# Opening of a hybrid attention/mLSTM diffusion step: x loaded, normalised and transposed ahead of the modulation weights, and modulated three row blocks at a time from SBUF

## The chip, the cores and the metric

The kernel runs on one core of a Trainium2 chip. TensorE (PE) multiplies matrices and transposes, VectorE (DVE), ScalarE (ACT) and GpSimd (POOL) do elementwise work, and SyncE (SP) issues nearly all transfers between HBM and SBUF. The metric is device time of one execution in microseconds, given as the median of several runs. Beside the timed runs there is one profiled execution, from which all rows of the profile come.

## The reference, cut to what matters

One layer of a diffusion backbone works on 128 context tokens and 1024 latent tokens of width 1024: nine row blocks of 128 tokens. The parts which the change touches are the first ones:

```python
m = jax.nn.silu(cond) @ w_ada_l + b_ada_l              # six rows of 1024: sh1, sc1, g1, sh2, sc2, g2
h = rmsnorm(x, norm1_w) * (1 + sc1) + sh1              # context tokens use c_ctx, latent tokens use c
aq, ak, av, mq, mk, mv, mo, mg = jnp.split(h @ w_in, SPLIT_POINTS, axis=-1)
```

Behind them come attention over context and latent keys, a bidirectional mLSTM of four heads over chunks of 128 tokens, a merged output projection, and a SwiGLU feed-forward of width 2816. All arithmetic is in float32.

## The kernel before, in words

The nine row blocks (block 0 is the context, blocks 1 to 8 the latent tokens) are grouped three to a chunk c, so that c=0 holds blocks 0, 1, 2. Everything multiplies from a transposed layout: `hT[c]` holds h of three blocks with the 1024 features over eight groups k of 128 partitions, split into an f16 high part `hTh` and an f16 low part `hTl`, and weights are split likewise into pairs; three f16 products then stand for one float32 product.

The opening goes as follows.

- Small rows (c, c_ctx, biases, norm weights) are loaded on ACT's queue and transposed; SiLU gives `silp` (L286 to L301).
- SP loads block 0 of x (L268) and then sixteen tiles of 512 KB of the modulation weights w_ada (L273): eight for the shift, eight for the scale. They lie in a pool of their own, `awp`, which is closed behind them. Then come the cached keys and values and the gate bias (L377 to L379), the raw weights of the key/value/gate projection `kvg` (L194, tile `kraw`), blocks 1 to 8 of x (L393, L395), and the raw weights of head 0 (L194, tile `iraw`).
- `normalise` squares a block on ACT (L331), takes the reciprocal root by three Newton steps of small DVE operations (`rsqrt`, L125 to L131), and multiplies x in place on DVE (L334). `transposed` turns a block on PE into two PSUM banks of four 128-column pieces each (L114). Block 0 goes through both before the modulation weights are read.
- For shift and then for scale PE multiplies `silp` with each of the eight tiles (L318, into `wi`), two evictions (L356) and small products (L324) bring the result into columns, and `modulation` adds the bias and multiplies the norm weight (L310, L313). Then a bound over scale and shift is made a power of two (`hsc`, L364 to L366 and L162 to L165), and both are multiplied with it (L369).
- For each block in turn, eight pieces of 128 columns are read from PSUM, multiplied by scale and shifted into a tile `full`: k = 1, 4, 7 on ACT (L417), the others on DVE (L420). Each half block is cast to f16 (half 0 on ACT, L426; half 1 on DVE, L428), and POOL subtracts to give the low part (L135, `sub`).
- `Scaled` prepares a weight: `ready` loads it, takes absolute sums on ACT (L199), reduces them (L201), multiplies the bound with `hsc` (L202), and lets `power_scale` find a power of two through a PE transpose and a PE broadcast (L172 to L177). `pairs` then makes high and low parts: ACT scales and casts (L216, or L219 and L220), DVE (L217) or POOL (L135) makes the low part. For kvg this is emitted behind block 0 with a priority of 300, all low parts on DVE.
- `linear_tok` is the projection: for each group of blocks, eight k and three products (L488 to L490). For kvg it runs over five groups, `PAIRS`, with 272 columns, and `evac_kvg` writes keys, values and gates (L497, L498, L501). The preparation of head 0 (`steps`) is woven among it, 8 steps over 40 units. Behind it follows `head_project` of head 0 (L748 to L750 for q, by two chunks and then one).

The shared weight pool `wp` has tags with fixed numbers of buffers: `raw` 2, `whi` 5 and `wlo` 5, of 4 KB a partition each. Raw weights of the heads take `wlo`, finished pairs take `whi`.

The code gives only a program order and priorities. A planner simulates a timeline of the program and fixes each engine's order from it, so each engine runs its own list in order and waits on semaphores where the list says so. `hot(n)` raises the priority of what is emitted within it. What is emitted earlier usually comes earlier, but the planner may exchange operations which are ready at other times.

Of the kernel before, what the change touches and what calls it, by code (L numbers as in the profile page):

```python
# [22 lines left out]
NB = 9  # L23
# [22 lines left out]
def hybrid_step(ctx: ExitStack, tc: tile.TileContext, I: dict, O: dict):  # L46
# [55 lines left out]
    def bank():  # L102
        return psum["mm"].tile([P, 512], F32, name=nm("mm"), tag="mm")
# [76 lines left out]
    class Scaled:  # L180
# [5 lines left out]
        def ready(self):  # L186
# [15 lines left out]
            dve.tensor_tensor(out=t[:, 4:5], in0=t[:, 4:5], in1=hsc[:, 3:4], op=ALU.mult)  # L202
            yield from power_scale(gp, one1, t[:, 4:5], t[:, 6:8])
            dve.tensor_tensor(out=t[:, 8:9], in0=t[:, 6:7], in1=hsc[:, 3:4], op=ALU.mult)
            dve.tensor_scalar(out=t[:, 9:10], in0=t[:, 7:8], scalar1=P ** -0.5, scalar2=None, op0=ALU.mult)
            dve.tensor_scalar(out=t[:, 10:11], in0=t[:, 7:8], scalar1=0.5, scalar2=None, op0=ALU.mult)
            self.scale, self.inv, self.inv_k, self.inv_half = t[:, 8:9], t[:, 7:8], t[:, 9:10], t[:, 10:11]

        def pairs(self, dve_every=2):
            out = []  # L210
# [45 lines left out]
    es_w = ExitStack()  # L256
    awp = es_w.enter_context(tc.tile_pool(name="awp", bufs=1, side="right", reuse_waits="tile"))
# [9 lines left out]
    xs = [p0.tile([P, D], F32, name=f"x{b}") for b in range(NB)]  # L267
    dma(xs[0], xrow(0))  # L268
    ada_w = [[], []]
    for n in range(2):  # L270
        for k in range(KD):
            aw = awp.tile([P, D], F32, name=f"aw0_{n}_{k}")
            dma(aw, w_ada[k * P : (k + 1) * P, n * D : (n + 1) * D])  # L273
            ada_w[n].append(aw)
# [52 lines left out]
    def normalise(b0, n):  # L327
        ssx = p0.tile([P, CB], F32, name=f"ssx{b0}")
        for i in range(n):
            jk = p0.tile([P, D], BF16, name=nm("jk"), tag="jk", bufs=2)  # L330
            act(jk, xs[b0 + i], AF.Square, accum_out=ssx[:, i : i + 1])  # L331
        rs = rsqrt(p0, ssx[:, 0:n], n, 1.0 / D)
        for i in range(n):
            dve.tensor_scalar(out=xs[b0 + i], in0=xs[b0 + i], scalar1=rs[:, i : i + 1], scalar2=None, op0=ALU.mult)  # L334

    def transposed(b):
        pss = []
        for half in range(2):
            ps = bank()
            for j in range(4):  # L340
                k = half * 4 + j
                transpose(ps[:, j * P : (j + 1) * P], xs[b][:, k * P : (k + 1) * P])
            pss.append(ps)
        return pss

    normalise(0, 1)
    xT = [transposed(0)]

    for n, out in ((0, shift1), (1, scale1)):
        halves = [bankA(), bankA()]  # L350
        for k in range(KD):
            for j, pe in enumerate(halves):
                strip_products(pe, k, silp, ada_w[n][k][:, j * 512 : (j + 1) * 512], 2 * j)
        for j, pe in enumerate(halves):
            part = p0.tile([P, 512], F32, name=nm("part"), tag="part", bufs=2)
            (nc.scalar.copy if j == 0 else dve.tensor_copy)(part, pe)  # L356
            cols_from_strips(out, n, j, part, bankA)
    es_w.close()

    hp = ctx.enter_context(tc.tile_pool(name="hp", bufs=1, side="right", reuse_waits="tile"))  # L360
    hT = [hp.tile([P, 2, KD, CT], F16, name=f"hT{c}", tag=f"b{3 + c}") for c in range(NCH)]
    hTh, hTl = [t[:, 0] for t in hT], [t[:, 1] for t in hT]

    dve.tensor_reduce(out=hs2, in_=shift1, axis=AX.XY, op=ALU.max, apply_absolute_value=True)  # L364
    dve.tensor_reduce(out=hsc[:, 0:1], in_=scale1, axis=AX.XY, op=ALU.max, apply_absolute_value=True)
    dve.scalar_tensor_tensor(out=hsc[:, 0:1], in0=hsc[:, 0:1], scalar=float(D) ** 0.5, in1=hs2, op0=ALU.mult, op1=ALU.add)  # L366
    powers(hsc, P)
    for t in (scale1, shift1):
        dve.tensor_scalar(out=t, in0=t, scalar1=hsc[:, 2:3], scalar2=None, op0=ALU.mult)  # L369
    es_h = ExitStack()  # L370
    kvp = es_h.enter_context(tc.tile_pool(name="kvp", bufs=1, side="right", reuse_waits="tile"))
# [4 lines left out]

    dma(kall[:, 8], I["cache_k"][0, 0])  # L377
    dma(vall[:, 8], I["cache_v"][0, 0])
    dma(gbias, I["gate_bias"].rearrange("o g h -> o (g h)").to_broadcast([P, 16]))  # L379
    dve.memset(G, 0.0)  # L380

    Gv = G.rearrange("p t (d x) -> p d t x", d=2)

    def rows_of(j):
        return w_in[2 * j * P : (2 * j + 2) * P, :].rearrange("(a p) n -> p a n", p=P)

    kvg = Scaled([[(lambda v: v[:, :, 0:256], rows_of(j)[:, :, 512:768]),
                   (lambda v: v[:, :, 256:272], rows_of(j)[:, :, 2816:2832])] for j in range(4)], (2, 272),
                 [p0.tile([P, 544], F32, name=f"kraw{j}") for j in range(4)])
    kvg_steps = kvg.ready()  # L390
    next(kvg_steps)
    for b in range(1, CB):
        dma(xs[b], xrow(b))  # L393
    for b in range(CB, NB):
        dma(xs[b], xrow(b))  # L395
# [4 lines left out]

    groups_in = [head_group(h) for h in range(NH)] + [Scaled([[(full_view, rows_of(j)[:, :, 0:512])] for j in range(4)], (2, 512))]
    steps = groups_in[0].ready()
    next(steps)
    for c in range(NCH):
        if c > 0:
            normalise(c * CB, CB)
        for i in range(CB):
            b = c * CB + i
            cnd = 0 if b == 0 else 1
            if b in (1, 2):  # L410
                normalise(b, 1)
            for half, ps in enumerate(xT[b] if b < 1 else transposed(b)):
                full = p0.tile([P, 4, P], F32, name=nm("full"), tag="full", bufs=3)
                for j in range(4):
                    k = half * 4 + j
                    if k in (1, 4, 7):
                        act(full[:, j, :], ps[:, j * P : (j + 1) * P], AF.Identity,  # L417
                            scale=scale1[:, k, cnd : cnd + 1], bias=shift1[:, k, cnd : cnd + 1])
                    else:
                        dve.tensor_scalar(  # L420
                            out=full[:, j, :], in0=ps[:, j * P : (j + 1) * P],
                            scalar1=scale1[:, k, cnd : cnd + 1], scalar2=shift1[:, k, cnd : cnd + 1],
                            op0=ALU.mult, op1=ALU.add)
                hi = hTh[c][:, half * 4 : half * 4 + 4, i * P : (i + 1) * P]
                if half == 0:
                    nc.scalar.copy(hi, full)  # L426
                else:
                    dve.tensor_copy(hi, full)  # L428
                sub(hTl[c][:, half * 4 : half * 4 + 4, i * P : (i + 1) * P], full, hi, "pool")
            if b == 0:  # L430
                with hot(300):
                    emit(kvg_steps)
                    kvg_pairs = kvg.pairs(1)
# [69 lines left out]
    weave(linear_tok(kvg_pairs, 0, 272, evac_kvg), steps, 40, 8)  # L503
# [1016 lines left out]
```

## Time and profile before

| what | value |
|---|---|
| median of 3 runs (lowest, highest) | 1628.43 us (1624.75, 2519.12) |
| the profiled execution's own time | 1623.65 us |
| its span, first to last instruction | 1621.9 us |
| mean granted TensorE clock | 0.973 |
| busy in the span: PE, DVE, ACT, POOL | 1513.3, 955.2, 730.7, 602.4 us |
| moved by DMA | 232.71 MB |

In rows of the timeline the columns are start in us, duration in us, engine, line and operation, output and inputs, count, and in brackets the idle time before it with what ended it. In grouped rows the last columns are busy time in us, mean duration in ns, and idle time before with its releasers. In rows of one tile or line the three numbers behind the count are the smallest, median and largest duration in ns. In rows of stretches each engine has its busy time and, in brackets, its instructions; behind them stand the granted clock, the DMA engines' mean busy share and GB/s. Durations of neighbouring operations on one engine overlap a little, since an operation starts before the one ahead has been drained; the distance between starts is then the cost.

### The profile page before, as it was taken

What the parts mean: (1) busy time and instruction counts of PE and PEld (TensorE: products, weight loads), DVE (VectorE), ACT (ScalarE), POOL (GpSimd) and SP (SyncE); (2) the same over time, 40 slices, a digit from 0 to 9 for tenths busy, and PEclk for the clock granted to TensorE, in tenths of its full rate; (3) what the DMA queues carried; (4) which work ended last, traced back from release to release, by engine and by line L of the source; (5) the groups of instructions that cost most, each with busy time, mean ns of one, the idle gap of its engine ahead of it and who ended that gap; (6) DMA issues with size and microseconds to landing.
All of it is one profiled execution on the core that took longest, in us unless ns stands there. A gap on an engine that the chain in (4) does not pass through costs nothing. (4 is left out here: it accounts for less than half of the span.)

```text
span 1621.9 us, 23339 instructions
## 1 busy us (share of the span) xinstructions
PE 1513.3 (93%) x8688; PEld 1256.2 (77%) x8688; DVE 955.2 (59%) x1887; ACT 730.7 (45%) x1251; POOL 602.4 (37%) x363
## 2 busy tenths in 40 slices
PE   5899999899679867999999999999999999999996
PEld 2755666576347656998989999898898989899995
DVE  3844355847876667577663546777664474332445
ACT  3744343444444455545643344565552453333332
POOL 0411021413343414443445354443344444544443
PEclk8899999999889979999999999999999999999998
DMA  9345363302245755777763556787684445535441
GB/s 353 121 143 134 99 143 63 97 6 44 87 163 120 194 119 113 172 184 177 183 174 115 148 153 215 189 179 177 153 185 126 130 141 177 150 124 149 143 129 67
DMA packets 386311, 232.71 MB, mean 143 GB/s; under 512 B 169910, under 2 KB 346502, under 8 KB 386198
## 3 DMA queue, kind: packets, MB, share of 16 engines
q1 hardware_dynamic: 384342, 228.04, 52.6%
q10 hardware_dynamic: 1856, 3.19, 0.6%
q8 instruction: 68, 1.11, 0.3%
q14 instruction: 45, 0.37, 0.1%
HBM read 181.16 MB, written 11.69 MB: 119 GB/s over the span
## 5 line engine op out<-in xcount | busy, mean ns | idle before, releaser
L135 POOL TENSOR_TENSOR wlo<-raw,whi 128x1024 fp32r<-128x1024 f32 x146 | 360.9, 2476 | 435.6 <-ACT whi L152 404.5
L152 ACT CAST whi<-raw 128x1024 fp32r<-128x1024 f32 x219 | 224.1, 1025 | 357.9 <-DMA raw<-in_w_gu_dram 126.8
L1288 PE MATMUL mm<-aTl,whi 128*128 128x384 f32 (+2 forms) x1088 | 363.6, 334 | 0.7 <-POOL aTl L135 0.7
L1289 PE MATMUL mm<-aTh,wlo 128*128 128x384 f32 (+2 forms) x1088 | 363.4, 334 | 0.0
L1287 PE MATMUL mm<-aTh,whi 128*128 128x384 f32 (+2 forms) x1088 | 362.2, 335 | 0.8 <-DVE tn L1315 0.8
L1288 PEld LDWEIGHTS mm<-aTl,whi 128*128 128x128 f32 x1088 | 204.9, 188 | 1.7 <-POOL aTl L135 0.9
L1287 PEld LDWEIGHTS mm<-aTh,whi 128*128 128x128 f32 x1088 | 204.5, 188 | 2.2 <-DVE tn L1315 1.4
L1289 PEld LDWEIGHTS mm<-aTh,wlo 128*128 128x128 f32 x1088 | 204.9, 188 | 0.2
L135 DVE TENSOR_TENSOR wlo<-raw,whi 128x1024 fp32r<-128x1024 f32 (+1 forms) x73 | 86.7, 1188 | 145.5 <-ACT whi L152 145.3
L1106 PE MATMUL mm<-whi,hl 128*128 128x512 f32 x372 | 147.0, 399 | 1.4 <-DVE tn L1315 1.3
L1107 PE MATMUL mm<-wlo,hl 128*128 128x512 f32 x372 | 147.6, 398 | 0.0
L1108 PE MATMUL mm<-whi,hl 128*128 128x512 f32 x372 | 144.7, 397 | 0.7 <-POOL hl L135 0.7
L1023 DVE SCALAR_TENSOR_TENSOR pl<-pr,st,ph 128x1152 f16<-128x1152 f32 (+1 forms) x72 | 111.9, 1556 | 52.7 <-ACT ph L1022 51.0
L1019 ACT ACTIVATE pr<-S,st 128x1152 f32<-128x1152 f32 (+1 forms) x72 | 81.2, 1128 | 114.8 <-DVE st L1018 108.5
L488 PE MATMUL wi<-ipair,hT 128*128 128x384 f16 (+2 forms) x392 | 127.5, 326 | 2.9 <-ACT ipair L216 2.8
L489 PE MATMUL wi<-ipair,hT 128*128 128x384 f16 (+2 forms) x392 | 127.4, 325 | 0.0
L490 PE MATMUL wi<-ipair,hT 128*128 128x384 f16 (+2 forms) x392 | 126.8, 324 | 0.0
L135 POOL TENSOR_TENSOR hl<-tn,hl 128x384 fp32r<-128x384 f32 x66 | 82.8, 1256 | 106.9 <-ACT hl L1319 106.0
L1096 DVE TENSOR_TENSOR x<-x,t 128x512 f32<-128x512 f32 x102 | 116.7, 1167 | 0.8
L1315 DVE SCALAR_TENSOR_TENSOR tn<-tn,mm 128x384 f32<-128x384 f32 (+2 forms) x68 | 36.7, 540 | 136.3 <-PE mm L1289 93.5
L1016 PE MATMUL S<-kst,qT 128*128 128x384 f32 (+1 forms) x400 | 87.2, 353 | 13.5 <-ACT pr L1019 13.4
L1018 DVE TENSOR_REDUCE st<-S 128x1 f32<-128x1152 f32 (+1 forms) x72 | 88.8, 1233 | 16.7 <-PE S L1016 16.5
(353 smaller groups left out, 2639.5 us busy)
## 6 DMA issues: line engine op xcount, KB each, us to landing
raw<-in_w_gu_dram SPq DMA_DIRECT2D x132, 512.0 KB
raw<-in_w_down_dram SPq DMA_DIRECT2D x60, 512.0 KB
a<-in_w_ada_dram SPq DMA_DIRECT2D x32, 512.0 KB
gl<-g_d SPq DMA_DIRECT2D x36, 256.0 KB
aw<-in_w_ada_dram SPq DMA_DIRECT2D x16, 512.0 KB
iraw<-in_w_in_dram SPq DMA_DIRECT2D x32, 256.0 KB
raw<-in_w_out_dram SPq DMA_DIRECT2D x15, 512.0 KB
x<-in_x_sample_dram SPq DMA_DIRECT2D x13, 512.0 KB
```

The costliest lines, as they stand in the source:

```text
L135: (dve if eng == "dve" else pool).tensor_tensor(out=out, in0=full, in1=hi, op=ALU.subtract)
L152: nc.scalar.copy(hi[:, :n], raw[:, :n])
L488: mm(ps[:, :n], ah, wh[:, k % 2, c0 : c0 + n], start=(k == 0), stop=False)
L489: mm(ps[:, :n], ah, wl[:, k % 2, c0 : c0 + n], start=False, stop=False)
L490: mm(ps[:, :n], al, wh[:, k % 2, c0 : c0 + n], start=False, stop=(k == KD - 1))
L1096: eng.tensor_tensor(out=x1[:, cs], in0=x1[:, cs], in1=t, op=ALU.add)
L1106: mm(ps, ah, wh[:, k % 2, :], start=(k == 0), stop=False)
L1107: mm(ps, ah, wl[:, k % 2, :], start=False, stop=False)
L1108: mm(ps, al, wh[:, k % 2, :], start=False, stop=(k == nk - 1))
L1287: mm(ps, wh[:, k, :], th[:, k, :], start=(k == 0), stop=False)
L1288: mm(ps, wh[:, k, :], tl[:, k, :], start=False, stop=False)
L1289: mm(ps, wl[:, k, :], th[:, k, :], start=False, stop=(k == KD - 1))
```

## The change

- SP loads x in chunks of three blocks: chunks 0 and 1 (six blocks) ahead of all modulation weights, chunk 2 behind the raw kvg weights, into six x buffers instead of nine. The cached keys and values and the gate bias come behind chunk 2.
- The pool `awp` is gone. The sixteen modulation weight tiles go into `wp`: the first five into `wlo`, the next five into `whi`, two into `raw`, and the last four into `whi` again, so that these four wait for earlier tiles to be read.
- `turned(c)` takes the place of `normalise` and `transposed`: three squares, one rsqrt chain for three blocks, and per block the multiplication, eight transposes and two evictions (half 0 on ACT, half 1 on DVE) into `xT[c]` in SBUF. `turned(0)` is emitted ahead of the shift, `turned(1)` between shift and scale, `turned(2)` behind the modulation of c=1.
- `modulated(c)` multiplies and shifts `xT[c]` in place: for c=0 two pieces per k (128 columns with the context's values, 256 with the latent's) on DVE; for c=1 and c=2 one piece of 384 columns per k, k = 3 and 7 on ACT, the others on DVE. Then, per half, one cast of 1536 columns on ACT and one subtraction of 1536 columns, on POOL for half 1 of c=1 and c=2, on DVE otherwise.
- The bound `hsc` has a priority of 60, `modulated(0)` of 40; the priority of 300 at the kvg pairs is gone.
- The power of two of a weight no longer has `hsc` in it; the new method `inverse` multiplies `hsc` into the factor of the evictions.
- The kvg projection runs over six groups of blocks, and `steps` is woven over 48 units.

```diff
-            dve.tensor_tensor(out=t[:, 4:5], in0=t[:, 4:5], in1=hsc[:, 3:4], op=ALU.mult)
             yield from power_scale(gp, one1, t[:, 4:5], t[:, 6:8])
-            dve.tensor_tensor(out=t[:, 8:9], in0=t[:, 6:7], in1=hsc[:, 3:4], op=ALU.mult)
...
+            self.scale, self.t = t[:, 6:7], t
+        def inverse(self):
+            t = self.t
+            dve.tensor_tensor(out=t[:, 8:9], in0=t[:, 7:8], in1=hsc[:, 3:4], op=ALU.mult)
...
-    dma(xs[0], xrow(0))
...
+    def load_x(c):
+        xs = [p0.tile([P, D], F32, name=nm("x"), tag="x", bufs=2 * CB) for _ in range(CB)]
+        for i in range(CB):
+            dma(xs[i], xrow(c * CB + i))
+        return xs
+    def load_ada(n):
+        tiles = []
         for k in range(KD):
-            aw = awp.tile([P, D], F32, name=f"aw0_{n}_{k}")
+            tag, bufs = (("wlo", 5), ("whi", 5), ("raw", 2), ("whi", 5))[(0, 0, 0, 0, 0, 1, 1, 1, 1, 1, 2, 2, 3, 3, 3, 3)[n * KD + k]]
+            aw = wp.tile([P, 1024], F32, name=nm("aw"), tag=tag, bufs=bufs)
             dma(aw, w_ada[k * P : (k + 1) * P, n * D : (n + 1) * D])
...
+    xs = [load_x(0), load_x(1), None]
+    ada_w = [load_ada(0)]
...
+    def turned(c):
+        ssx = p0.tile([P, CB], F32, name=f"ssx{c}")
+        for i in range(CB):
             jk = p0.tile([P, D], BF16, name=nm("jk"), tag="jk", bufs=2)
+            act(jk, xs[c][i], AF.Square, accum_out=ssx[:, i : i + 1])
+        rs = rsqrt(p0, ssx, CB, 1.0 / D)
+        xT = hp.tile([P, KD, CT], F32, name=nm("xT"), tag=f"b{c}")
+        for i in range(CB):
+            dve.tensor_scalar(out=xs[c][i], in0=xs[c][i], scalar1=rs[:, i : i + 1], scalar2=None, op0=ALU.mult)
+            for half in range(2):
+                ps = bank()
+                for j in range(4):
+                    k = half * 4 + j
+                    transpose(ps[:, j * P : (j + 1) * P], xs[c][i][:, k * P : (k + 1) * P])
+                (nc.scalar.copy if half == 0 else dve.tensor_copy)(
+                    xT[:, half * 4 : half * 4 + 4, i * P : (i + 1) * P], ps.rearrange("p (j x) -> p j x", j=4))
+            yield
+        xTs.append(xT)
...
+    xTs = []
+    emit(turned(0))
+    ada_w.append(load_ada(1))
+    emit(ada_cols(0, shift1))
+    emit(turned(1))
+    kvg_steps = kvg.ready()
+    next(kvg_steps)
+    xs[2] = load_x(2)
...
+    steps = groups_in[0].ready()
     next(steps)
+    emit(ada_cols(1, scale1))
+    with hot(60):
...
+    def modulated(c):
+        xT = xTs[c]
+        for half in range(2):
+            ks = slice(half * 4, half * 4 + 4)
+            for k in range(half * 4, half * 4 + 4):
+                for lo, hi, cnd in ((0, P, 0), (P, CT, 1)) if c == 0 else ((0, CT, 1),):
+                    v = xT[:, k, lo:hi]
+                    if c > 0 and k % 4 == 3:
+                        act(v, v, AF.Identity, scale=scale1[:, k, cnd : cnd + 1], bias=shift1[:, k, cnd : cnd + 1])
                     else:
+                        dve.tensor_scalar(out=v, in0=v, scalar1=scale1[:, k, cnd : cnd + 1], scalar2=shift1[:, k, cnd : cnd + 1],
+                                          op0=ALU.mult, op1=ALU.add)
+            nc.scalar.copy(hTh[c][:, ks], xT[:, ks])
+            sub(hTl[c][:, ks], xT[:, ks], hTh[c][:, ks], "pool" if c > 0 and half == 1 else "dve")
+    with hot(40):
+        modulated(0)
+    emit(kvg_steps)
+    kvg_pairs = kvg.pairs(1)
+    modulated(1)
+    emit(turned(2))
+    modulated(2)
     es0.close()
...
-    weave(linear_tok(kvg_pairs, 0, 272, evac_kvg), steps, 40, 8)
+    weave(linear_tok(kvg_pairs, 0, 272, evac_kvg, [(0, 1), (2,), (3, 4), (5,), (6, 7), (8,)]), steps, 48, 8)
```

More of the change, by code (lines that the diff above doesn't have):

```diff
@@ L353, in hybrid_step @@
                 strip_products(pe, k, silp, ada_w[n][k][:, j * 512 : (j + 1) * 512], 2 * j)
+            yield
         for j, pe in enumerate(halves):
@@ L357, in hybrid_step @@
             cols_from_strips(out, n, j, part, bankA)
[L358 to L371, printed above, removed]
+        yield
     kall = kvp.tile([P, 10, NKV, HD], F32, name="kall")
```

95 lines of the change are left out of this document (25 added, 70 removed).

## The prediction, on record before the result

> **What bounds the kernel now.** I read the page's 40 slices first: TensorE (PE) is 90% busy or more in most slices; less so in the first two and in a few between 280 and 650 us. The change touches only what happens before the first head's projection, which is slices 1 and 2, so I then read busy time by stretches of that opening, then the timeline and the groups by line inside it.
>
> ```profile
> PE   5899999899679867999999999999999999999996
> ...
> 0.00:20.00 20.00, 12.91 (x67) 4.79 (x69) 5.84 (x30) 3.23 (x5) 1.01 (x7) 1.00 0.90 352
> ...
> 33.50:39.60 6.10, 0.97 (x4) 0.68 (x4) 5.76 (x32) 6.10 (x14) 2.20 (x2) 0.50 1.02 410
> 39.60:45.20 5.60, 4.45 (x20) 3.27 (x20) 5.57 (x20) 5.60 (x12) 0.08 (x1) 0.50 1.10 357
> 45.20:50.00 4.80, 2.95 (x24) 2.17 (x22) 4.70 (x22) 4.80 (x13) 1.16 (x1) 0.99 1.10 328
> 55.00:60.00 5.00, 2.93 (x19) 2.11 (x18) 4.94 (x17) 2.43 (x7) 0.89 (x1) 0.89 0.11 30
> 60.00:65.00 5.00, 5.00 (x36) 3.92 (x34) 4.05 (x10) 3.19 (x8) 3.59 (x4) 0.77 0.02 3
> ```
>
> The columns are the stretch, its length, busy time of PE, of its weight load, of DVE, ACT and POOL, the granted clock and DMA. From 33.5 to 60 DVE is busy in all but a few tenths, while PE is idle for long parts or runs at half clock (0.50). From 60 on PE is full. So the opening is set by the arrival of the modulation weights until about 30 us, by DVE until about 60, and by PE after it.
>
> ```profile
> 78.98 0.28 PE L490 MATMUL wi<-ipair,hT 128*128 128x272 f16 x1
> ...
> 82.45 0.28 PE L490 MATMUL wi<-ipair,hT 128*128 128x272 f16 x1
> 82.57 0.33 PE L748 MATMUL wi<-hT,ipair 128*128 128x384 f16 x1
> ```
>
> 82.57 us is the point I count to: the last matmul of the key/value/gate projection (kvg) is followed at once by the first of head 0. Behind it PE is 90% busy or more until 280 us, so what moves this point moves the end by about as much. Between the two L490 rows lie 30 matmuls: 3.47/30 = 0.1157 us each at full clock. The projection has 9 blocks x 8 x 3 = 216, hence 25.0 us. It now takes from 39.58 to 82.57, 43.0 us. The rest is 64 transposes of x, half clock, and idle time.
>
> **The change, part by part. (a) The order of the loads.** Five x tiles come ahead of the modulation weights, and all these loads share SP's queue.
>
> ```profile
> 4.96 1.06 ACT L331 ACTIVATE jk<-x 128x1024 bf16<-128x1024 f32 x1
> ...
> 25.84 1.05 PE L318 MATMUL wi<-aw,silp 128*32 128x512 f32 x4 [0.31 <-DMA aw<-in_w_ada_dram]
> ...
> 29.61 0.17 DVE L310 TENSOR_TENSOR scale<-wi,bcol 128x8 f32<-128x8 f32 x1 [0.53 <-PE wi L324]
> ...
> 31.37 0.66 ACT L199 ACTIVATE jk<-kraw 128x544 bf16<-128x544 f32 x1 [0.37 <-DMA kraw<-in_w_in_dram]
> ...
> 32.15 0.16 DVE L201 TENSOR_REDUCE isc<-isc 128x1 f32<-128x4 f32 x1 [2.38 <-ACT jk L199]
> 32.22 0.16 DVE L313 TENSOR_TENSOR scale<-scale,ncol 128x8 f32<-128x8 f32 x1
> ...
> 33.52 0.23 DVE L369 TENSOR_SCALAR shift<-shift,hsc 128x16 f32<-128x16 f32 x1
> 33.66 0.15 DVE L202 TENSOR_TENSOR isc<-isc,hsc 128x1 f32<-128x1 f32 x1
> ...
> 37.19 0.14 DVE L177 COPY isc<-mm 128x2 f32<-128x2 f32 x1
> ```
>
> The first x is there at 4.96, the sixteenth weight tile at 25.84: 1.305 us for a tile of 512 KB. Five more in front put the last weight tile at 32.4. Today the scaled vectors are ready 7.9 us after it, at 33.75; but between 29.78 and 32.15 DVE stood behind L201, whose reduction waited for the kvg weights. The new code puts the maximum of scale and shift ahead with a priority of 60 and no longer makes the kvg scale depend on it, so I take that 2.3 us out: 32.4 + 5.6 = 38.0. If L201 still goes first, 40.3. Modulation therefore starts 4.2 us later than now (bounds: 0.3 later if the planner leaves x3 to x5, 3 x 1.3 us, behind the weights, and 6.5 if L201 goes first). The reuse of weight tiles costs nothing: the last four wait until PE has read the sixth to ninth tile, which land at 11.5 + 6 x 1.305 = 19.3 up to 23.2, while their own turn in the queue begins at 11.5 + 12 x 1.305 = 27.2; that slack of about 7 us is the cover, and each us beyond it would move 38.0 by as much. The x6 to x8, cache and iraw loads come later by at most the same 6.5, and land before c=2 and head 0 need them.
>
> **(b) What leaves the stage.** Squares, rsqrt, normalising and 48 of the 72 transposes now lie in the time when PE and DVE wait for weights. Before 30 us DVE is busy 5.84 of the first 20 us, so the 12 us added there (two rsqrt chains of 1.9, 6 x 0.75, 6 half evictions) fit. New are 18 evictions from PSUM to xT, 512 wide, like L356 at 0.69 us on DVE and 0.59 on ACT; 12 of them are hidden in the same way.
>
> ```profile
> L420 DVE TENSOR_SCALAR full<-mm,scale,shift 128x128 f32<-128x128 f32 x45 | 16.2, 400 | 0.4 <-POOL hT L135 0.4
> L428 DVE CAST hT<-full 128x512 f16<-128x512 f32 x9 | 6.7, 749 | 0.6 <-ACT full L417 0.4
> L334 DVE TENSOR_SCALAR x<-x,ry 128x1024 f32<-128x1024 f32 x8 | 5.7, 750 | 0.0
> L217 DVE SCALAR_TENSOR_TENSOR ipair<-kraw,isc,ipair 128x544 f16<-128x544 f32 x4 | 3.1, 776 | 0.0
> ...
> L356 DVE COPY part<-wi 128x512 f32<-128x512 f32 x2 | 1.4, 692 | 12.2 <-PE wi L318 12.2
> L535 DVE TENSOR_SCALAR gb<-ga 128x128 f32<-128x128 f32 x1 | 0.2, 227 | 0.3 <-ACT ga L534 0.3
> L709 DVE TENSOR_SCALAR mwh<-mwh 128x512 f32<-128x512 f32 x1 | 0.4, 418 | 0.0
> L135 DVE TENSOR_TENSOR wlo<-raw,whi x73: 684/1225/1560, 458.2 to 1588.5; 128x1024 fp32r<-128x1024 f32 x67, 128x512 fp32r<-128x512 f32 x6
> L220 ACT CAST ipair<-iraw 128x1024 f16<-128x1024 f32 x2 | 2.1, 1030 | 0.0
> ```
>
> **(c) The modulation from SBUF.** The 72 pieces of 128 columns from PSUM, 45 of them on DVE and 27 (k = 1, 4, 7) on ACT, become, per c: for c=0 eight pairs of 128 and 256 columns on DVE, for c=1 and 2 six DVE and two ACT pieces of 384. From SBUF, 128 columns took 0.227 us (L535) and 512 took 0.418 (L709), so 256 is 0.29 and 384 is 0.36. That is 8 x 0.52 = 4.2, and 6 x 0.36 = 2.1 for each of the others, against 16.2 now. The nine DVE casts of 6.7 us go to ACT: six of 1536 columns at 1.03 x 1.5, or 1.5 each. Four of six subtractions go from POOL to DVE: 1.225 us at 1024 and 0.684 at 512 give 1.77 at 1536, 7.1 in all. DVE after 38.0 is then: modulation 8.4, subtractions 7.1, kvg low parts 3.1, kvg scale 1.5 (ten of 0.15), rsqrt (twelve of 0.16), normalising and evictions of c=2 1.9 + 2.3 + 2.1, gates and head 0's scale some 4.6 (32 small operations of about 0.14, the shortest above): 31 us, where it is now busy 16.0 of the 16.5 us from 33.5 to 50, 4.9 of 5 from 55 and 4.05 of 5 from 60. DVE is done at about 69, ahead of PE, so it ceases to be the bound.
>
> **(d) When kvg can start and end.** In c=0 the DVE modulates until 42.2, and subtracts the two halves until 45.7. The kvg weights land at 31.37 now, 5.5 us behind the last modulation weight, so at 37.9; 0.85 for the last absolute sum, 3.7 for the scale (L202 at 33.66 to L177's end at 37.33), ACT's high part of 0.74 and DVE's 0.78: the first pair is whole between 44 (DVE takes it between the subtractions) and 46.5 (behind them). I take 46, because modulated(0) alone has the raised priority.
>
> ```profile
> 39.58 0.39 PE L488 MATMUL wi<-ipair,hT 128*128 128x272 f16 x1 [2.79 <-ACT ipair L216]
> ...
> 42.88 0.43 PE L489 MATMUL wi<-ipair,hT 128*128 128x272 f16 x1
> ...
> 43.56 0.43 PE L489 MATMUL wi<-ipair,hT 128*128 128x272 f16 x1
> ...
> 44.01 0.43 PE L488 MATMUL wi<-ipair,hT 128*128 128x272 f16 x1
> ...
> 66.19 0.60 PE L114 MATMUL mm<-ident,x 128*128 128x128 f32 x4
> 66.63 0.28 PE L490 MATMUL wi<-ipair,hT 128*128 128x272 f16 x1
> ...
> 81.35 1.15 ACT L216 ACTIVATE ipair<-iraw,isc 128x1024 f16<-128x1024 f32 x1
> ...
> 82.53 5.28 DVE L217 SCALAR_TENSOR_TENSOR ipair<-iraw,isc,ipair 128x1024 f16<-128x1024 f32 x2 [3.42 <-ACT ipair L216]
> ```
>
> From there PE has 25.0 for kvg, 24 transposes of c=2 at 0.11 (four from 66.19 to 66.63), 2.6, head 0's scale 0.5, and a cold start: after an idle stretch the matmuls lie 0.225 apart (43.56 to 44.01); the stretches above show a clock of 0.50 from 33.5 to 45.2 and 0.99 behind it, so some 4 us after the first transposes at 41 were slow, and 4 us cost 2.0. 46 + 30.1 = 76.1. For waits on c=1 and c=2 I add 1.0 (none to 7.0, see the rivals): 77.1, 5.5 us before 82.57. The groups become six; the last is block 8 alone, so the first kvg pair gives its buffer back 2.1 us before head 0 instead of 4.2. Head 0 needs its second pair 2.0 us after its start and that pair costs 1.15 on ACT and up to 2.7 on DVE: just in time, nothing added, at worst 1 us.
>
> The profiled execution took 1623.65 us, 1.75 around its span of 1621.9. 1623.65 - 5.5 = **1618 us**. The median shown, 1628.43, is 4.8 above that execution, and the lowest run, 1624.75, 1.1 above: the spread is nearly the size of the gain. A change of 2% is about what a measurement of this kernel can tell from none.
>
> **The rivals. A larger gain.** The pairs come at 44, transposes of c=2 fall into PE's wait before that, and c=1 and 2 are always ready: 44 + 25.0 + 2.5 = 71.5, a gain of 11, 1613 us. That DVE has 10 us less to do speaks for it; that three stages of 1536 columns must pass from DVE to ACT and back before PE can go on speaks against.
>
> **No gain: POOL shuts DVE out.**
>
> ```profile
> L135 POOL TENSOR_TENSOR hT<-full,hT 128x512 f16<-128x512 f32 x18 | 20.8, 1160 | 55.7 <-DVE rt L129 35.9 <-ACT hT L426 10.2 <-DVE hT L428 9.7
> ...
> 53.44 1.20 POOL L135 TENSOR_TENSOR hT<-full,hT 128x512 f16<-128x512 f32 x1 [0.18 <-ACT hT L426]
> 53.46 0.14 DVE L130 SCALAR_TENSOR_TENSOR rt<-rt,rv 128x3 f32<-128x3 f32 x1
> ...
> 53.64 1.01 DVE L131 SCALAR_TENSOR_TENSOR ry<-rt,ry 128x3 f32<-128x3 f32 x1
> ```
>
> Of two three-column DVE operations the one took 0.14 as POOL began, and the next took 1.01 and ended with POOL's subtraction, while L420, which reads PSUM, keeps its 0.40 throughout. POOL keeps two subtractions, of 1536 columns: 3 x 1.16 = 3.5 us each. If all modulation, normalising and rsqrt behind them wait, 7.0 us go onto DVE's path and the gain is gone: 77.1 - 1.0 + 7.0 = 83.1, 1624 us. Against it: POOL now works 20.8 us in this stage, and 7.0 after. The Trainium skill, SBUF — State Buffer, section "SBUF: two separate sides", says that such a DVE operation and GpSimd take one pair of ports as an exclusive lock for a whole instruction; the row agrees, and by it every piece of modulation from SBUF can be shut out, which those from PSUM could not.
>
> **Slower: the later start is not won back.** Modulation starts 4.2 us later, and c=0 reaches PE in pieces of three blocks rather than of one. If kvg, from its first pair at 46, is paced as it is now from 42.88 to 82.57 (39.7 us), because the chain DVE to ACT to DVE or POOL of each c shows in full, head 0 starts at 85.7, 3.1 late, 1627 us. It decides from 8.6 us of PE idle within kvg on top of the 1.0. For it: PE's idle time today (1.85 us of 45.2 to 50, 2.07 of 55 to 60) falls where DVE is full, so PE follows that chain. Against: three chains of about 2.1 + 1.5 + 1.8 us, each under 8.3 us of matmuls of the block group ahead.
>
> **That it doesn't do what it says.** The planner orders every engine by its own timeline; x3 to x5 could still go behind weights. Then modulation starts up to 3.9 us sooner and the larger gain's number holds; it is counted there.
>
> **Chances.** Forecast 50% (1614 to 1622), larger gain 18%, no gain 17%, slower 15%. The range 1609 to 1630 takes in the larger gain's number with 4 us of later replanning below and the slower one's with 3 above, and leaves out some 2 in 10. None of the cases reaches 2% (33 us) by itself: the whole stage offers only 43.0 - 25.0 us. Faster 0.03, same 0.94, slower 0.03, the tails for a replanned rest of the kernel.
>
> **What would show it.** Last modulation weight at about 32.4 and scaled vectors at 38; the DVE pieces from SBUF at 0.23 to 0.36; kvg's matmuls 0.1157 apart with only 24 transposes among them; head 0's first L748-like matmul near 77. It is wrong if that point stands at 82 or later, if DVE's pieces take over 1 us beside POOL, if the weights land much after 33, or if the rest, counted from that point, changes its length by more than some us.

## The result and the profile after

| | before | after |
|---|---|---|
| median (lowest to highest), us | 1626.59 (1623.26 to 2519.12), 4 runs | 1646.28 (1640.27 to 1649.85), 4 runs |
| profiled execution / its span, us | 1623.65 / 1621.9 | 1640.27 / 1638.5 |
| scaled vectors ready, us from the span's start | 33.75 | 60.71 |
| first matmul of head 0 (L748, now L756) | 82.57 | 99.62 |
| from there to the end of the span | 1539.3 | 1538.9 |

One of the four runs before took 2519.12 us, and the ratio is that of the other seven runs. It is 1.0124, with a 95% interval of 1.0092 to 1.0156: the change makes the kernel slower by about 1.2%. The forecast was 1618 us, faster by 5.5, in a range of 1609 to 1630. Of the 16.6 us which the span grew, 17.05 lie ahead of head 0's first matmul and none behind it. So the opening alone has to be read. The profiled execution of the kernel after is the fastest of its four; the medians differ by 19.7 us, so some 3 us of the loss stand in no profile.

In the 40 slices of the page for the kernel after, PE's first two slices were 5 and 8 and are 4 and 5; behind them six slices stand below 9, where seven did.

```profile
PE   4599999999868967999999999999999999999996
```

The next view is the kernel after by stretches of 20 us (columns as in the prediction). From 20 to 60 us PE is busy 24 of 40 us, and DVE, which in the kernel before was full from 33.5 on, is busy 18.4 of 40. DVE is full only from 60 to 80.

```profile
20.00:40.00 20.00, 12.30 (x83) 5.92 (x82) 5.83 (x17) 9.95 (x22) 0.00 (x0) 0.77 1.06 358
40.00:60.00 20.00, 11.77 (x59) 7.38 (x59) 12.52 (x38) 11.94 (x18) 2.16 (x2) 0.76 0.67 237
60.00:80.00 20.00, 9.83 (x61) 6.60 (x62) 19.97 (x45) 12.79 (x16) 8.79 (x2) 0.62 0.17 48
```

What they wait for shows on the queue that issues the loads. In the kernel before, SP issues all sixteen modulation weight tiles (`aw`) one behind the other:

```profile
1.65 14.18 SPq L273 DMA_DIRECT2D aw<-in_w_ada_dram  x16
```

This is SP in the timeline of the kernel after: start of the first issue, time over which the issues stretch, and how many there are.

```profile
6.88 10.68 SPq L285 DMA_DIRECT2D aw<-in_w_ada_dram  x12
18.52 9.68 SPq L194 DMA_DIRECT2D kraw<-in_w_in_dram  x8
28.69 0.81 SPq L277 DMA_DIRECT2D x<-in_x_sample_dram  x2
...
31.83 0.93 SPq L194 DMA_DIRECT2D iraw<-in_w_in_dram  x2
...
33.76 5.92 SPq L194 DMA_DIRECT2D iraw<-in_w_in_dram  x7
39.77 0.64 SPq L285 DMA_DIRECT2D aw<-in_w_ada_dram  x1
...
42.17 1.13 SPq L285 DMA_DIRECT2D aw<-in_w_ada_dram  x2
...
44.68 0.47 SPq L285 DMA_DIRECT2D aw<-in_w_ada_dram  x1
```

Only twelve tiles are issued one behind the other. The thirteenth is issued at 39.77 and the sixteenth at 44.68, behind the raw kvg weights, chunk 2 of x, the cache, and nine loads of head 0's weights. These four are the tiles that take over `whi` buffers. The next rows are PE, DVE, ACT and POOL in the same timeline.

```profile
43.17 4.53 PE L114 MATMUL mm<-ident,x 128*128 128x128 f32 x20 [6.27 <-DVE x L352]
47.63 1.16 PE L334 MATMUL wi<-aw,silp 128*32 128x512 f32 x4
...
53.50 1.05 PE L334 MATMUL wi<-aw,silp 128*32 128x512 f32 x4 [0.48 <-DMA aw<-in_w_ada_dram]
...
57.24 1.82 DVE L329 TENSOR_TENSOR scale<-scale,ncol 128x8 f32<-128x8 f32 x1
...
60.48 0.23 DVE L415 TENSOR_SCALAR shift<-shift,hsc 128x16 f32<-128x16 f32 x1
60.76 4.72 DVE L430 TENSOR_SCALAR xT<-xT,scale,shift 128x128 f32<-128x128 f32 x16
65.37 8.32 ACT L432 CAST hT<-xT 128x1536 f16<-128x1536 f32 x6
65.52 4.76 DVE L430 TENSOR_SCALAR xT<-xT,scale,shift 128x384 f32<-128x384 f32 x12
66.88 0.41 PE L496 MATMUL wi<-ipair,hT 128*128 128x272 f16 x1 [8.98 <-ACT hT L432]
...
70.53 1.75 DVE L135 TENSOR_TENSOR hT<-xT,hT 128x1536 f16<-128x1536 f32 x1
71.02 8.79 POOL L135 TENSOR_TENSOR hT<-xT,hT 128x1536 f16<-128x1536 f32 x2 [11.94 <-ACT hT L432]
72.33 4.53 DVE L135 TENSOR_TENSOR hT<-xT,hT 128x1536 f16<-128x1536 f32 x1
```

The last product with a modulation weight starts at 53.50, where it was 25.84. PE had even turned 20 pieces of chunk 2 ahead of the thirteenth tile's product (47.63). The scaled vectors follow at 60.71 instead of 38.0. From there it is 38.9 us to head 0, where the prediction had 77.1 - 38.0 = 39.1. That these two agree is in part luck: in the kernel after, the kvg scale and the transposes of chunk 2 are done ahead of the vectors (by 37.1 and 49.4), and the prediction had both behind them.

### The profile page after: what moved, and what is told of

It is laid out like the page before. It is cut to its first block, busy times and chain, and to the rows that moved or that the text cites. A ratio compares the mean times of both kernels' runs of the same rounds, so it can differ in the third digit from the quotient of the medians.

```text
span 1638.5 us, 23274 instructions
## 1 busy us (share of the span) xinstructions
PE 1518.5 (93%) x8688; PEld 1257.4 (77%) x8688; DVE 957.4 (58%) x1844; ACT 733.0 (45%) x1234; POOL 590.9 (36%) x347
## 5 line engine op out<-in xcount | busy, mean ns | idle before, releaser
L1031 DVE SCALAR_TENSOR_TENSOR pl<-pr,st,ph 128x1152 f16<-128x1152 f32 (+1 forms) x72 | 110.0, 1529 | 40.2 <-ACT ph L1030 39.2
L1024 PE MATMUL S<-kst,qT 128*128 128x384 f32 (+1 forms) x400 | 90.6, 362 | 22.8 <-ACT pr L1027 22.6
```

## The experiments

The question was what puts the weights at 53.50. My theory: the last four tiles depend on a buffer's release, and with that they lose their place in the order. The rivals: the five x tiles ahead are the price; the modulation in wider pieces and POOL's lock are; or the replanned rest of the kernel. All profiled executions in one table (start of the last modulation weight's products, or of the unbroken run of them that ends with it; scaled vectors ready; head 0's first matmul; from there to the end):

| kernel | products | vectors | head 0 | behind it | span | ratio to before, 95% |
|---|---|---|---|---|---|---|
| before | 25.84 | 33.75 | 82.57 | 1539.3 | 1621.9 | |
| after | 53.50 | 60.71 | 99.62 | 1538.9 | 1638.5 | 1.0124 (1.0092 to 1.0156) |
| e1_own | 31.56 | 40.00 | 82.00 | 1529.3 | 1611.3 | 0.9910 (0.9887 to 0.9934) |
| e11_recycle_early | 41.77 | 51.85 | 91.61 | 1544.6 | 1636.2 | 1.0074 (1.0045 to 1.0103) |
| e2_before_recycled | 43.69 | 51.63 | 90.34 | 1544.3 | 1634.6 | one run |
| e8_pool_queue | 55.92 | 64.92 | 103.81 | 1546.8 | 1650.6 | one run |
| e3_before_xfirst | 33.54 | 39.04 | 81.84 | 1550.1 | 1631.9 | one run |
| e4_own_x3late | 30.09 | 36.43 | 91.20 | 1545.7 | 1636.9 | 1.0074 (1.0050 to 1.0098) |
| e5_own_no_pool | 31.71 | 40.28 | 82.95 | 1539.1 | 1622.1 | one run |
| e10_own_cast_dve | 32.09 | 40.02 | 83.16 | 1547.0 | 1630.2 | 1.0019 (1.0001 to 1.0037) |
| n2_groups_only | 25.77 | 33.81 | 83.11 | 1541.1 | 1624.2 | 1.0001 (0.9978 to 1.0024) |

**e1_own: the last four tiles in buffers of their own.** The kernel after, with the last four tiles in the later buffers of `hT` (tags b3 and b4), which are free until the modulation writes them (`[...]` stands for the table of indices).

```diff
-            tag, bufs = (("wlo", 5), ("whi", 5), ("raw", 2), ("whi", 5))[...]
-            aw = wp.tile([P, 1024], F32, name=nm("aw"), tag=tag, bufs=bufs)
+            if n * KD + k >= 12:
+                if n * KD + k in (12, 15):
+                    own = hp.tile([P, 3, 1024], F32, name=nm("awh"), tag="b3" if k == 4 else "b4")
+                aw = own[:, (k - 4) % 3, :]
+            else:
+                tag, bufs = (("wlo", 5), ("whi", 5), ("raw", 2))[...]
+                aw = wp.tile([P, 1024], F32, name=nm("aw"), tag=tag, bufs=bufs)
```

> The changed kernel, but the last four modulation weight tiles lie in buffers of their own (those of hT, which are not in use yet) instead of buffers that earlier tiles must first give back. Theory (the four recycled tiles stand behind other loads in SP's queue): the last tile lands at 32 to 34, the scaled vectors are ready at 38 to 40 instead of 60.7, head 0 starts at 77 to 80 instead of 99.6, and the time is 1616 to 1622. Rival (the modulation from SBUF in pieces of three blocks, with POOL shutting DVE out, is the longer stage, and the late weights only fill its shadow): head 0 still starts at 90 or later, and the time stays above 1632.

The median is 1613.75 us (1609.78 to 1615.02, four runs), 0.9% below before. The timeline of e1_own:

```profile
6.64 10.74 SPq L290 DMA_DIRECT2D aw<-in_w_ada_dram  x12
18.30 1.58 SPq L290 DMA_DIRECT2D awh<-in_w_ada_dram  x2
20.80 1.57 SPq L290 DMA_DIRECT2D awh<-in_w_ada_dram  x2
23.58 10.21 SPq L194 DMA_DIRECT2D kraw<-in_w_in_dram  x8
...
31.56 2.94 PE L339 MATMUL wi<-awh,silp 128*32 128x512 f32 x16
...
39.77 0.23 DVE L420 TENSOR_SCALAR shift<-shift,hsc 128x16 f32<-128x16 f32 x1
...
44.75 1.25 DVE L435 TENSOR_SCALAR xT<-xT,scale,shift 128x384 f32<-128x384 f32 x3
...
46.46 1.05 ACT L199 ACTIVATE jk<-iraw 128x1024 bf16<-128x1024 f32 x1
...
46.61 0.86 PE L501 MATMUL wi<-ipair,hT 128*128 128x272 f16 x3 [6.90 <-ACT hT L437]
...
48.55 2.83 ACT L437 CAST hT<-xT 128x1536 f16<-128x1536 f32 x2
...
50.06 3.42 DVE L135 TENSOR_TENSOR hT<-xT,hT 128x1536 f16<-128x1536 f32 x2
...
51.44 0.41 PE L501 MATMUL wi<-ipair,hT 128*128 128x272 f16 x1 [3.29 <-ACT hT L437]
...
54.91 3.26 POOL L135 TENSOR_TENSOR hT<-xT,hT 128x1536 f16<-128x1536 f32 x1 [53.37 <-ACT hT L437]
55.20 3.04 DVE L127 TENSOR_SCALAR ry<-rh 128x3 int32<-128x3 int32 x1
```

All sixteen tiles are issued ahead of `kraw`, the sixteen products of the last four stand in one run, and the vectors are ready at 40.0. That takes 20.7 of the 22.7 us away by which (a) was off, and at head 0 17.6 us, more than the opening had lost. So the reuse of buffers is the cause of the loss in the opening. But head 0 comes at 82.0, not at the 77 to 80 that I had expected. Six kvg products run at 46.6, then PE waits until 51.44 for the second of the two casts from 48.55, which stand behind two absolute sums of head 0 (L199). The first product that reads a low part of `hT` (L503) starts at 51.87, just behind the first of the two subtractions from 50.06, and DVE comes to these only behind pieces of c=1 (44.75) and low parts of kvg. That this version beats the kernel before is due to the time behind head 0, which is 10.0 us shorter; see below.

**e2_before_recycled: the reuse alone, in the kernel before.**

```diff
-            aw = awp.tile([P, D], F32, name=f"aw0_{n}_{k}")
+            i = n * KD + k
+            i = i if i < 12 else i - 7
+            aw = awp.tile([P, D], F32, name=nm("aw0"), tag=f"aw{i}")
```

> The kernel before, with one edit: the last four modulation weight tiles take the buffers of the sixth to ninth instead of their own. Theory of the queue: these four are issued in between and behind the kvg weights and x (the last one behind all x and a part of head 0's weights), so the last tile lands near 42 instead of 25.8, the scaled vectors come at about 50 instead of 33.8, and head 0 starts at 90 to 96 instead of 82.6; 1631 to 1638. Rival (recycling alone is harmless, the length of the stage behind it makes the loss): head 0 within 2 us of 82.6, 1622 to 1627.

One run, 1636.41 us. In its timeline the last tile is again issued far back, behind the first head 0 weights, and PE waits 9.22 us for it:

```profile
31.11 5.39 SPq L194 DMA_DIRECT2D iraw<-in_w_in_dram  x3
36.59 1.14 SPq L275 DMA_DIRECT2D aw<-in_w_ada_dram  x1
...
43.69 1.92 PE L320 MATMUL wi<-aw,silp 128*32 128x512 f32 x4 [9.22 <-DMA aw<-in_w_ada_dram]
...
46.48 2.08 DVE L336 TENSOR_SCALAR x<-x,ry 128x1024 f32<-128x1024 f32 x3
```

The vectors come 17.9 us late without any other part of the change. Head 0 comes only 7.8 us late. What fits with that is that DVE normalises x meanwhile: the last normalising starts at 46.48, ahead of the vectors (51.63). In the kernel before it starts 22 us behind them (33.75):

```profile
55.98 2.08 DVE L334 TENSOR_SCALAR x<-x,ry 128x1024 f32<-128x1024 f32 x3
```

**e8_pool_queue: the same reuse, but the four loads issued from POOL's empty queue.**

```diff
-            dma(aw, w_ada[k * P : (k + 1) * P, n * D : (n + 1) * D])
+            (nc.gpsimd.dma_start if n * KD + k >= 12 else dma)(aw, w_ada[k * P : (k + 1) * P, n * D : (n + 1) * D])
```

> The changed kernel, its buffers recycled as they are, but the last four modulation weight tiles issued from POOL, which has nothing else to do before 57 us, so that SP's order cannot hold them back. Theory (the place in SP's order is what costs, not the wait for the buffers): they are issued when PE has read the earlier tiles, at 27 to 31, share the DMA engines with the kvg weights and x, the scaled vectors are ready at 42 to 46 instead of 60.7, and head 0 starts at 83 to 88 instead of 99.6. Rival (the wait for the buffers itself is what costs): scaled vectors at 55 or later and head 0 within 4 us of 99.6.

One run, 1652.36 us: no better, so "SP's queue alone" falls. The vectors, at 64.92, and head 0, 4.2 us beyond 99.6, come about where the rival had them. Its reason, the wait for the buffers, is not what the timeline shows:

```profile
25.70 0.72 POOL L285 DMA_DIRECT2D aw<-in_w_ada_dram  x1 [24.15 <-PE wi L334]
27.71 1.05 POOL L285 DMA_DIRECT2D aw<-in_w_ada_dram  x2 [1.29 <-PE wi L334]
31.38 0.53 POOL L285 DMA_DIRECT2D aw<-in_w_ada_dram  x1 [2.61 <-PE wi L334]
35.97 0.68 SPq L277 DMA_DIRECT2D x<-in_x_sample_dram  x1
...
46.98 3.67 PE L114 MATMUL mm<-ident,x 128*128 128x128 f32 x16 [8.07 <-DVE x L352]
50.59 1.92 PE L334 MATMUL wi<-aw,silp 128*32 128x512 f32 x4
...
55.92 1.06 PE L334 MATMUL wi<-aw,silp 128*32 128x512 f32 x8
```

The next line is from the rows of the tile `aw` in the same kernel: the time from issue to landing of these four loads.

```profile
DMA to landing us min/median/max: 6.1/7.0/7.8
```

The brackets on POOL show that these issues waited for PE's reading, so they give the time of each release: 25.70 to 31.38. The loads are issued at least 13 us earlier than in the kernel after and have landed by 31.38 + 7.8 = 39.2 at the latest, but PE comes to the last two at 55.92. For PE's own list has the products behind the transposes of chunk 2, and those wait until 46.98 for DVE's normalising of chunk 2, whose last tile SP issues at 35.97. The lateness of the four tiles is written into the order of more than one engine. The Trainium skill says that issuing DMAs from several engines only saves the sequencer's issue time (Trainium Kernel Development and Optimization, section "Key Constraints"), and that PE's queue can pull weight loads ahead of matmuls that are in flight (TensorE: Matmul & The Clock Gate, section "Architectural detail: the array is 16× 32×32, not 1× 128×128"). The rows contradict neither: the earlier issue by itself brought no product forward, and no product passed the waiting transposes in those 8.07 us.

**e11_recycle_early: reuse of buffers that come free earlier.**

```diff
-            tag, bufs = (("wlo", 5), ("whi", 5), ("raw", 2), ("whi", 5))[...]
+            tag, bufs = (("wlo", 5), ("whi", 5), ("raw", 2), ("wlo", 5))[...]
```

> The changed kernel with one thing changed: the last four modulation weight tiles take over the buffers of the first to fourth tile instead of the sixth to ninth, so they depend on a release as before, but on one some 7 us earlier. In SP's list the first two of them now stand right behind the kvg weights, two x blocks and the cache, ahead of all head 0 weights, the other two behind one x block and one other load; in the changed kernel all four stood behind seven or more head 0 loads. My theory (the place in the planned order, set by when the planner expects the buffer free, is the price): the last tile is read at 37 to 44 us instead of 53.5, the scaled vectors are ready at 44 to 51 instead of 60.7, head 0 starts 39 to 43 behind them, at 84 to 93 instead of 99.6; time 1621 to 1637 by a rest of 1535 to 1543, with 8 us more either way if the rest is ordered anew again. Rival one (any dependence on a release is put behind everything that is free, whichever buffer it is): vectors at 57 to 63, head 0 at 97 to 102, time 1636 to 1648. Rival two (only the bare extra wait for the release counts, and the order has nothing to do with it): the buffers are free long before, so the vectors come at 38 to 41 as with buffers of their own, head 0 at 80 to 83.

The median is 1637.67 us (1637.08 to 1639.45, four runs). The timeline of e11_recycle_early:

```profile
31.32 0.85 SPq L285 DMA_DIRECT2D aw<-in_w_ada_dram  x2
...
34.16 1.00 SPq L285 DMA_DIRECT2D aw<-in_w_ada_dram  x2
...
41.77 3.21 PE L334 MATMUL wi<-aw,silp 128*32 128x512 f32 x8 [2.06 <-DMA aw<-in_w_ada_dram]
44.92 2.50 PE L114 MATMUL mm<-ident,x 128*128 128x128 f32 x16
47.25 0.95 PE L340 MATMUL wi<-strip_sel,part 128*128 128x2 f32 x8
```

With the release some 8 us earlier (PE reads the first tile at 15.78 here, and the sixth at 23.92 in the kernel after) all four loads stand ahead of head 0's weights, and the products ahead of the transposes of chunk 2. PE has read the first four tiles by 20.0, and the loads are issued from 31.32 on: it is for their place on SP that they wait, no longer for the buffer. Vectors at 40.0, 51.9 and 60.7, head 0 at 82.0, 91.6 and 99.6 for no release, an early one and a late one: the loss grows with the lateness of the release, and both rivals miss (rival one had 57 to 63, rival two 38 to 41). The vectors are 0.9 us beyond the 44 to 51 that I had written, since the small products of L340 stand behind 16 transposes. The span falls by only 2.3, because the rest is 5.7 longer, and the median is just above the 1621 to 1637 that I had written.

**e3_before_xfirst: five x tiles ahead, nothing else, in the kernel before.**

```diff
-    dma(xs[0], xrow(0))
+    for b in range(2 * CB):
+        dma(xs[b], xrow(b))
...
-    for b in range(1, CB):
-        dma(xs[b], xrow(b))
-    for b in range(CB, NB):
+    for b in range(2 * CB, NB):
         dma(xs[b], xrow(b))
```

> The kernel before, with blocks 1 to 5 of x issued ahead of the modulation weights and nothing else. Theory: the last weight tile lands at 32.4, the scaled vectors are ready 4 to 6.5 us later than the 33.8 of before, and head 0 starts 2 to 6.5 us late, 1625 to 1631. Rival (the order of x is what costs the changed kernel its 17 us): 1635 or more.

One run, 1633.72 us. Vectors 5.3 us later, head 0 0.7 us earlier (81.84), where I had expected it 2 to 6.5 us later: the x tiles ahead of the weights cost the opening nothing. The total lies between what I expected (up to 1631) and the rival's 1635, and all that it has above the kernel before is behind head 0 (1550.1).

**e4_own_x3late: e1_own, with x3 to x5 behind the modulation weights.**

```diff
-    xs = [load_x(0), load_x(1), None]
+    xs = [load_x(0), None, None]
...
+    xs[1] = load_x(1)
```

> As e1_own, with blocks 3 to 5 of x issued behind all modulation weights. Theory: last weight tile at 28.5, scaled vectors 3.9 us before e1_own's; if the squares, transposes and evictions of c=1 still fit beside the other work, head 0 starts 2 to 4 us before e1_own's, 1613 to 1619. Rival: they land in the stage that DVE fills, and the time is equal to e1_own's or up to 4 us above.

The median is 1639.32 us (1638.28 to 1640.79, four runs). The vectors are earlier by 3.6 and head 0 is later by 9.2. The timeline of e4_own_x3late shows why: 24 transposes, which wait for the normalising of chunk 1, now stand on PE ahead of the small matmuls of the kvg scale, which ends only behind 57.74.

```profile
46.78 4.54 PE L114 MATMUL mm<-ident,x 128*128 128x128 f32 x24 [12.59 <-DVE x L357]
...
57.74 0.55 PE L176 MATMUL mm<-pv,one 1*128 1x2 f32 x2 [6.30 <-DVE pv L165]
```

So chunk 1 ahead of the weights is worth 9 us in this form of the kernel, and the rival was right, more strongly than written. The median is 25.6 us above e1_own's, where the rival had up to 4; the 16.4 us beyond head 0's 9.2 lie behind head 0 and are not explained by these rows.

**e5_own_no_pool and e10_own_cast_dve: what holds e1_own at 82.** All subtractions on DVE; and, in the second, the casts of c=0 on DVE.

```diff
-            sub(hTl[c][:, ks], xT[:, ks], hTh[c][:, ks], "pool" if c > 0 and half == 1 else "dve")
+            sub(hTl[c][:, ks], xT[:, ks], hTh[c][:, ks], "dve")
```

> e1_own with all six subtractions on DVE, none on POOL. If POOL's exclusion of DVE is a price on the path (in e1_own a DVE operation of 3 columns took 3.04 us beside POOL), head 0 starts 1 to 3 us before e1_own's 82.0. If the subtraction is as long on DVE's path as the exclusion was (1.76 against 3.0), and PE sets the end, head 0 stays within 1 us of 82.0. The time of the whole may differ by up to 10 us either way by the order of later stages.

```diff
-            nc.scalar.copy(hTh[c][:, ks], xT[:, ks])
+            (dve.tensor_copy if c == 0 else nc.scalar.copy)(hTh[c][:, ks], xT[:, ks])
```

> e1_own with the two casts of c=0 on DVE instead of ACT, so that c=0 no longer passes from DVE to ACT and back. In e1_own the first long run of kvg matmuls begins at 51.4 where the prediction had 46, because ACT's second cast of c=0 stood behind head 0's absolute sums. If that is the lost 5 us, the run begins at 46 to 49 and head 0 starts at 77 to 80. If instead DVE's total of work sets it, both stay within 1.5 us of e1_own's 51.4 and 82.0.

Head 0 at 82.95 (one run, 1623.85 us) and at 83.16 (median 1628.59, 1622.67 to 1633.43, ten runs). POOL's lock is seen in e1_own (3.04 us for three columns), but without POOL head 0 is not earlier; and the way through ACT is not the lost 5 us either. In e10_own_cast_dve kvg's unbroken run begins at 53.62, later than both readings had it (46 to 49, or within 1.5 us of 51.4), and what PE waits for there is a subtraction on DVE:

```profile
53.62 0.63 PE L503 MATMUL wi<-ipair,hT 128*128 128x272 f16 x2 [3.99 <-DVE hT L135]
```

In both forms, then, DVE comes late to the subtractions of c=0. No run here puts them ahead.

**n2_groups_only: six groups and the weave over 48 units, in the kernel before.**

```diff
-    weave(linear_tok(kvg_pairs, 0, 272, evac_kvg), steps, 40, 8)
+    weave(linear_tok(kvg_pairs, 0, 272, evac_kvg, [(0, 1), (2,), (3, 4), (5,), (6, 7), (8,)]), steps, 48, 8)
```

> The kernel before with one small part of the change: kvg over six groups of blocks and the weave over 48 units. Head 0 should start within 1 us of 82.6. Theory (a change of the opening's program order makes the planner order PE anew from about 440 us on, and that alone is worth up to 10 us either way): the stretch from head 0's start to the end differs from before by more than 2 us although nothing behind head 0 was edited. Rival (the rest keeps its length): the whole is within 2 us of before.

The median is 1626.06 us over ten runs (1617.30 to 1634.79): no difference that can be measured. This edit is not the loss. It was also meant to test whether a small edit of the opening alone changes the length of the rest by more than 2 us: it changed it by 1.8 (1541.1 against 1539.3), so the rival holds here.

**What stays open: the time behind head 0.** It goes from 1529.3 to 1550.1 over kernels whose code there is the same. First starts in four profiled executions, from the rows of L1016 and L1106 (first attention product and first product of the output projection, by the lines of the kernel before; in the others they stand 8 or 13 lines further on), with the stretches between them:

| kernel | head 0 to L1016 | L1016 to L1106 | L1106 to the end |
|---|---|---|---|
| before | 368.7 | 229.9 | 940.7 |
| after | 367.7 | 233.3 | 937.9 |
| e1_own | 364.9 | 224.4 | 940.0 |
| e11_recycle_early | 366.6 | 239.8 | 938.2 |

The last 940 us hardly differ; the middle stretch, the attention, differs by 15 us. My guess is that an edit of the opening changes the order that is planned for the attention, but n2_groups_only did not show it, and no other run tests it. Runs of one kernel also spread by up to 17 us (n2_groups_only), so one execution says little about this stretch. The four runs of e1_own do lie below all seven runs of the kernel before that were timed beside them (at most 1615.02 against at least 1621.65). Where its 10 us behind head 0 come from is open, so its advantage over the kernel before is not a proof that the idea of the change pays.

## Why the prediction was wrong

**(a) The order of the loads: this step failed.** The sentence was "The reuse of weight tiles costs nothing", with "that slack of about 7 us is the cover". The term was 0; it measured 60.7 - 40.0 = 20.7 us in the vectors and 99.6 - 82.0 = 17.6 at head 0. Two things were wrong in it. First, I set the release against the tiles' turn in the queue as counted by landings (27.2). What waits for the release is the issue, and SP runs far ahead: it has issued the twelfth tile by 6.88 + 10.68 = 17.56, and with buffers of their own the last four from 18.30 to 22.37 (e1_own). The releases come at 25.70 to 31.38 (e8_pool_queue), not at 19.3 to 23.2, since PE reads the tiles between transposes and not as they land. So there was no slack of 7 us but a gap of 7 to 9. Second, I priced the reuse only as a wait in its place ("each us beyond it would move 38.0 by as much"); by that the gap would have cost about 9 us, an estimate from these two runs. The wait was not kept in place: the order of SP and of PE was planned around it, with other loads and other transposes ahead, so the last tile was issued at 44.68, 13.3 us behind its release, and read 8.8 us later still.

The other terms of (a) held: with buffers of their own the vectors come at 40.0 (forecast 38.0, and 40.3 for L201 in the way, where it stands at 37.76), and with five x tiles alone at 39.0.

**(b) What leaves the stage: right.** In the kernel after the squares, rsqrt, evictions and transposes of c=0 and c=1 are done before 30 us, and DVE is busy 5.83 us from 20 to 40. This part is worth something: in e3_before_xfirst, where five blocks are normalised ahead of the vectors and the modulation is the old one, DVE is busy 35.2 us from the vectors to head 0 against 42.75 in the kernel before, and that stage is 6.0 us shorter (42.8 against 48.8).

**(c) The modulation: sizes right, the worth wrong.** 16 pieces in 4.72 us (forecast 4.2), twelve of 384 columns in 4.76, 0.40 each (0.36), casts 8.32/6 = 1.39 (1.5), free subtractions 1.75 (1.77). But the stage from the vectors to head 0 is hardly shortened by the new form: 38.9 in the kernel after against 38.7 in e2_before_recycled, both with late vectors, and 42.0 in e1_own against 42.8 in e3_before_xfirst, both with vectors at 39 to 40 (single executions). In e1_own PE is busy 31.6 of the 42.0 us, in e3_before_xfirst 36.3 of the 42.8: it has less to do in the new form and waits more. The prediction took a full DVE from 33.5 to 60 for the bound and put 1.0 us on PE's waits for c=1 and c=2; it did not see that what leaves DVE can come back as such a wait.

**(d) kvg and head 0: 82.0 where 77.1 was forecast, with the weights in time.** Of the 4.9 us, 2.0 are the later vectors. kvg's unbroken run starts at 51.4 (forecast 46). The sum had DVE subtract the two halves of c=0 until 45.7, behind its modulation alone; in e1_own the modulation ends at 44.8 and the first two subtractions end at 53.5, with pieces of c=1 and kvg's low parts in between, and ACT does two absolute sums of head 0 between its first cast and the next (46.46 to 48.55). From the start of that run the 30.6 us to head 0 were forecast as 31.1. What would bring the start to 46 is open: two attempts (e5_own_no_pool, e10_own_cast_dve) did not.

**The rivals.** "Slower" came true in its sign, by another mechanism: it let the later start stand at 4.2 us and a slow kvg decide; the start was 27 us late, and kvg was not slow. POOL's exclusion is there, and each case costs DVE somewhat less than the 3.5 us written (3.04 and 4.53 us for operations of some 0.16 and 1.75); it is not on the path to head 0 in e1_own. "That it doesn't do what it says" named the planner and x3 to x5; x went where the code says, and the weights did not. The larger gain was far. The test written at the end of the prediction, "if the weights land much after 33", is the one that caught it.

## What to carry to other kernels

A load into a recycled buffer must be judged at its issue: set the time of the release against the time at which the queue would come to that load, not against the time at which its data would land. Where an order is planned ahead, as here, such a load may not only wait; it can lose its place on the issuing queue, and what uses it its place on the compute engine. Moving the issue to another queue did not mend that here; a buffer that is free earlier mended it in part, and a buffer of its own in full. And that an engine is full in a stretch does not yet say what it is worth to relieve it: compare the stage's length between kernels in which it starts at the same time before counting the relief as a gain.

## What the runs showed of the hardware that was not expected

DVE operations beside POOL's subtractions of 1536 columns are far longer than alone: 3.04 us for three columns in e1_own (it ends at 58.24, POOL's, 3.26 from 54.91, at 58.17), and 4.53 for a subtraction that takes 1.75 alone in the kernel after. POOL's operations grow too: the two there take 8.79 us together, 4.4 each, against 3.26 and 3.47 in e1_own. Even 128x8 values took 1.82 us beside a POOL subtraction of 1024 columns (L329, on the way to the scaled vectors), some 1.65 more than alone. The prediction had 3.5 us for each of POOL's two subtractions of `hT`, and nothing for those of the weights. In e1_own this lay beside the path, since without POOL head 0 did not come earlier; in the kernel after, the 1.65 us of L329 are a small part of the 20.7 by which the vectors were late.
